# Softmax normalised on the outputs of the value product, with the values' PSUM in another bank

## The chip, the cores and the metric

The kernel runs on one core of one Trainium2 chip. The metric is the device time of one execution in microseconds (us); less is better. TensorE (PE in the profile) multiplies matrices into PSUM, VectorE (DVE) and ScalarE (ACT) work element by element, GpSimd (POOL) and SyncE (SP) issue the transfers here.

## What is computed

One layer of a streaming encoder on 512 frames with 1,024 channels, in float32: a norm, one projection into three branches and their gates, the branches, a merge, and a feed-forward block. Branches A and C are softmax attentions with 8 heads of 64 value channels; branch B is a gated recurrence. What matters here is the softmax of A and C:

```python
s = jnp.einsum('bqhd,bkhd->bhqk', q_blk, k_band).astype(jnp.float32) * scale + bias
s = jnp.where(valid[None, None], s, -jnp.inf)
p = jax.nn.softmax(s, axis=-1).astype(v.dtype)
return jnp.einsum('bhqk,bkhd->bqhd', p, v_band)
```

Each query of each head has one sum of exponentials. The probabilities may be divided by it before the product with the values, or the product's output after it.

## The kernel before

The work is done transposed: channels lie on the partitions, frames along the free dimension, 512 to a tile. Each float32 factor is split into a rounded high part and a rest (`split`, L209: ScalarE makes the high part, VectorE the rest), and each large product is three matmuls. The order of TensorE is written out by hand: `manual_schedule` names TensorE alone, and the other engines' order is left to the framework. Between the steps of the attentions `fill(n)` (L302) puts n units of dense work, matmuls of the projections, out of a queue; their weights are loaded by GpSimd.

Stages that matter: branch C's attention (about 66 to 170 us), branch A's (170 to 275 us), then the recurrence of branch B. `attention` (L566) serves C and A. It goes through 32 steps, 8 heads (h) by 4 blocks of 128 queries (t), plus some at the end:

- `scores_step` (L516): TensorE computes the scores `sc` of one block against the keys up to it (128, 256, 384 or 512 columns); VectorE finds the extreme `mn` (L525 in C; in A it adds the bias table in the same operation, L529); ScalarE takes the exponential into `p` and its sum over the row into `sm` (L532). VectorE makes the reciprocal `ri` (L536) and scales `p` in place (L537). This `norm` is issued at the end of the step.
- `transpose_step` (L540), two steps later (`LAG`): TensorE transposes the blocks of `p` into a PSUM tile `tp` (L545), one to four blocks; ScalarE and VectorE split them into `pTh` and `pTl` (L210, L211).
- `value_step` (L554), once per head, four steps after its last scores: eight matmuls into a PSUM tile `av` (L561), with the high parts of the values giving its upper 64 rows and the rests its lower 64; ScalarE copies the lower half to `avl` (L563), VectorE adds the halves into the head's 64 rows of the output `yc` or `ya` (L564).
- `prep`: in C, while a pair of heads runs, the next pair's keys and queries are made (`prep_c`, L672: stages 1 to 3 use the PSUM tiles `pk`, `pn` and `pq`; VectorE reads `pq` in L693 and L694). In A, `prep_a` (L789) prepares the head after next, and loads its bias table from memory (L803, SP queue), which VectorE negates (L804).

PSUM: tag `tp` has two banks, taken in turn by the transposes and by `av`; tag `up` has one, taken in C by `pk`, `pn` and `pq`; `sc` has two, `acc` (dense work) three.

Behind A's last step the recurrence starts: `set_yx` splits the outputs of C (L869), the gates' matmuls run as dense work, and elementwise steps (L924 on) prepare B's products, some of which need ScalarE's `d` (L986).

Of the kernel before, what the change touches and what calls it, by code (L numbers as in the profile page):

```python
# [9 lines left out]
F32 = mybir.dt.float32  # L10
F32R = mybir.dt.float32r
I32 = mybir.dt.int32
AF = mybir.ActivationFunctionType
ALU = mybir.AluOpType
# [4 lines left out]
P = 128  # L19
NK = D // P  # L20
NST = S // P
# [112 lines left out]
def body(tc, ap, dbg=None):  # L134
    with ExitStack() as ctx:
        _body(ctx, tc, ap, dbg or {})


def _body(ctx, tc, ap, dbgo):
    nc = tc.nc  # L140
    V, A, G, T = nc.vector, nc.scalar, nc.gpsimd, nc.tensor
# [23 lines left out]
    def pup(n="up"):  # L165
        return ps.tile([P, S], F32, tag="up", name=n, bufs=1)

    def psc(n="sc"):
        return ps.tile([P, S], F32, tag="sc", name=n)

    def ptp(n="tp"):
        return ps.tile([P, S], F32, tag="tp", name=n)

    def fqt(n):
        return base.tile([P, S], F32, tag="fq", name=n, bufs=8)

    def yt(n):
        return base.tile([P, S], F32, tag="y", name=n, bufs=4)
# [16 lines left out]
    ident = base.tile([P, P], F32, name="ident")  # L195
# [75 lines left out]
    def convert():  # L271

        load()
        if raw:
            hi, src = raw.pop(0)
            lo = ws.tile([P, 1024], F32R, tag="wl", name="wl")
            A.activation(lo, f(hi), AF.Copy, scale=-1.0)  # L277
            G.dma_start(lo, src, accum_op=ALU.add)
            loaded.append((hi, lo))
            load()  # L280
# [14 lines left out]
    def units():  # L295
        while queue:
            yield from queue.pop(0)()
            count[1] += 1
# [3 lines left out]
    def fill(n):  # L302
        for _ in range(n):
            if next(dense[0], None) is None:
                dense[0] = units()
                if not queue:
                    return
            unit[0] += 1
            while due and unit[0] >= due[0]:
                due.pop(0)  # L310
                if len(loaded) < 2:
                    convert()
# [20 lines left out]
    with ExitStack() as st_ctx:  # L333
# [10 lines left out]
        for k in range(NK):  # L344
            t = st.tile([P, S], F32, tag="xt", name="xt", bufs=8)
# [75 lines left out]
        for i in range(4):  # L421
            t = fqt(f"c{i}")
# [90 lines left out]

    yraw = {}

    def scores_step(ab, t, scores, bias):  # L516
        n = (t + 1) * P
        sc = psc("sc")
        for i, (l, r) in enumerate(scores):
            T.matmul(sc[:, :n], l[:, t * P:(t + 1) * P], r[:, :n], start=i == 0, stop=i == len(scores) - 1)  # L520
        mn = ab.tile([P, 1], F32, tag="mn", name="mn", bufs=6)
        p = ab.tile([P, S], F32, tag="p", name="p", bufs=LAG + 1)
        if bias is None:
            V.memset(sc[0:64, n - 64:n], -NEG)
            V.tensor_reduce(mn, sc[:, :n], X, ALU.min)  # L525
            src = sc
        else:
            src = bias[1].tile([P, S], F32, tag="sb", name="sb", bufs=2)
            V.tensor_tensor_reduce(src[:, :n], sc[:, :n], bias[0][:, S - n:], 1.0, 3.0e38,  # L529
                                   ALU.add, ALU.min, accum_out=mn)  # L530
        sm = ab.tile([P, 1], F32, tag="sm", name="sm", bufs=6)
        A.activation(p[:, :n], src[:, :n], AF.Exp, bias=mn, scale=-1.0, accum_out=sm)  # L532
        ri = ab.tile([P, 1], F32, tag="ri", name="ri", bufs=6)

        def norm():
            V.reciprocal(ri, sm)  # L536
            V.tensor_scalar(p[:, :n], p[:, :n], ri, None, ALU.mult)  # L537
        return p, norm

    def transpose_step(par, t, p, pT):  # L540
        n = (t + 1) * P
        tp = ptp("tp")
        for kt in range(t + 1):
            o = kt if par == 0 else t - kt
            T.transpose(tp[:, o * P:(o + 1) * P], p[:, kt * P:(kt + 1) * P], ident)  # L545
        src = tp[:, :n].rearrange("p (k q) -> p k q", q=P)
        if par == 0:
            dh, dl = (x[:, 0:t + 1, t * P:(t + 1) * P] for x in pT)
        else:
            dh, dl = (bass.AP(tensor=x.tensor, offset=x.offset + (4 - t) * S,  # L550
                              ap=[list(x.ap[0]), [S + P, t + 1], [1, P]]) for x in pT)
        split(dh, dl, src)

    def value_step(ab, h, v2, pT, y):  # L554
        par = h % 2
        av = ptp("av")
        for kt in range(NST):
            w = v2[kt][:, h, :]
            for i, x in enumerate(pT):
                r = x[:, kt, kt * P:] if par == 0 else x[:, 4 - kt, :(NST - kt) * P]  # L560
                T.matmul(av[:, kt * P:], w, r, start=kt == 0 and i == 0, stop=kt == NST - 1 and i == 1)  # L561
        lo = ab.tile([64, S], F32, tag="avl", name="avl", bufs=1)
        A.copy(lo, av[64:128])  # L563
        V.tensor_tensor(y[par * 64:(par + 1) * 64], av[0:64], lo, ALU.add)  # L564

    def attention(ab, ops, prep, v2, pT, ys, na, nb, nd, lag=LAG):  # L566


        pend, vals = [], []
        order = [(h, t) for h in range(8) for t in range(NST)]  # L570
        for i in range(len(order) + lag + 2):
            norm = None
            if i < len(order):
                h, t = order[i]
                p, norm = scores_step(ab, t, *ops(h))
                pend.append((h, t, p))
            fill(na[i % len(na)] if i < len(order) else nd)
            if vals and (i % 2 or i >= len(order)):
                h = vals.pop(0)
                value_step(ab, h, v2, pT, ys[h // 2])  # L580
            if len(pend) > lag or (i >= len(order) and pend):
                h, t, p = pend.pop(0)
                transpose_step(h % 2, t, p, pT)
                if t == NST - 1:
                    vals.append(h)
            if norm:
                norm()
            if i < len(order):
                prep(*order[i])
            fill(nb[i % len(nb)] if i < len(order) else nd)  # L590
        assert not pend and not vals

    with ExitStack() as at_ctx:
        ab = at_ctx.enter_context(tc.tile_pool(name="attn", bufs=2, reuse_waits="tile"))
        pT = (ab.tile([P, 5, S], F32R, tag="pTh", name="pTh", bufs=1),
              ab.tile([P, 5, S], F32R, tag="pTl", name="pTl", bufs=1))
# [5 lines left out]
        with ExitStack() as c_ctx:  # L602
# [28 lines left out]
            v2 = []  # L631
            for s in range(NST):
# [3 lines left out]
                t = ab.tile([P, 8, P], F32R, tag="v2", name="v2", bufs=4)  # L636
# [19 lines left out]
            ys = [yt("yc") for _ in range(4)]  # L656
# [56 lines left out]
            for stage in range(4):  # L713
                prep_c(0, stage)
                fill(TUNE['c1'] if stage < 3 else TUNE['c2'])

            attention(ab, lambda h: ready(h % 2), next_c, v2, pT, ys, TUNE['ca'], TUNE['cb'], TUNE['cd'])
            for pr in range(4):
                dbg('yc', ys[pr], pr)
# [11 lines left out]
        with ExitStack() as a_ctx:  # L731
            app = a_ctx.enter_context(tc.tile_pool(name="apool", bufs=2, reuse_waits="tile"))
            v2 = []
            for s in range(NST):
                t = ab.tile([P, 8, P], F32R, tag="v2", name="v2a", bufs=4)
# [5 lines left out]
            ys = [yap.tile([P, S], F32, tag="ya", name="ya", bufs=4) for _ in range(4)]  # L741
# [47 lines left out]
            def prep_a(h):  # L789
# [20 lines left out]
            prep_a(1)  # L810
            fill(TUNE['a0'])
            attention(ab, lambda h: aops[h], lambda h, t: prep_a(h + 2) if t == 3 and h < 6 else None, v2, pT, ys,
                      TUNE['aa'], TUNE['ab'], TUNE['ad'])
            for pr in range(4):
# [4 lines left out]
    with ExitStack() as h_ctx:  # L819
# [11 lines left out]
        for i in range(LEAD + 1):  # L831
            a = hp.tile([P, 2, 256], F32R, name=f"qbh{i}", bufs=1)
# [321 lines left out]
    with ExitStack() as f_ctx:  # L1154
        fp = f_ctx.enter_context(tc.tile_pool(name="ffn", bufs=2, reuse_waits="tile"))

        def fw(n):
            return fp.tile([P, S], F32, tag="fw", name=n, bufs=3)
# [27 lines left out]
        for half in range(2):  # L1186
            rT = []
            for j in range(16):
# [3 lines left out]
                t = fw("t")  # L1192
# [10 lines left out]
            for m in range(NK):  # L1203
                pz = acc("p2")
                gemm(pz, stream(ap['w_ff2'][2 * half, m], eng=V), rT, NK, stop=half == 1)
                if half == 0:
                    gemm(pz, stream(ap['w_ff2'][1, m], eng=V), rT[8:], NK, start=False)
                    t = act.tile([P, S], F32, tag="act", name="y0")
# [36 lines left out]
        for sh in range(2):  # L1245
            n = slice(sh * 256, sh * 256 + 256)
# [33 lines left out]
```

## Time and profile before

| | |
|---|---|
| median of 3 runs | 961.58 us (961.29 to 964.99) |
| the profiled execution | 962.54 us |
| its span, first to last instruction | 960.8 us |
| mean granted clock of TensorE | 0.991 |
| TensorE, VectorE, ScalarE, GpSimd busy | 919.2, 595.2, 494.5, 183.2 us |

In rows of a timeline stand the start in us, the duration in us, the engine, the line, the operation, output <- inputs, shapes, and how many instructions the row merges; in brackets the idle time of the engine before it and the instruction that ended that. PE is the matmuls, PEld the loading of their stationary operand. Rows by windows give the stretch, its length, and for each engine the busy time with the number of instructions; then the granted clock (PEclk), the share of the DMA engines, and GB/s.

### The profile page before, as it was taken

What the parts mean: (1) busy time and instruction counts of PE and PEld (TensorE: products, weight loads), DVE (VectorE), ACT (ScalarE), POOL (GpSimd) and SP (SyncE); (2) the same over time, 40 slices, a digit from 0 to 9 for tenths busy, and PEclk for the clock granted to TensorE, in tenths of its full rate; (3) what the DMA queues carried; (4) which work ended last, traced back from release to release, by engine and by line L of the source; (5) the groups of instructions that cost most, each with busy time, mean ns of one, the idle gap of its engine ahead of it and who ended that gap; (6) DMA issues with size and microseconds to landing.
All of it is one profiled execution on the core that took longest, in us unless ns stands there. A gap on an engine that the chain in (4) does not pass through costs nothing.

```text
span 960.8 us, 12589 instructions
## 1 busy us (share of the span) xinstructions
PE 919.2 (96%) x4682; PEld 774.6 (81%) x4682; DVE 595.2 (62%) x1134; ACT 494.5 (51%) x911; POOL 183.2 (19%) x248
## 2 busy tenths in 40 slices
PE   8889999988998999999999999999999999999995
PEld 6578898977877788888778888888888888888995
DVE  6488888777878969788562554544322234446745
ACT  7557778777766667667552443443322234342311
POOL 4422101111144434342122013000000000000032
PEclk9999999999999999999999999999999999999998
DMA  6865445655666474758689623223223232322402
GB/s 198 212 136 124 89 82 114 138 116 121 139 131 134 102 165 104 161 125 193 136 209 203 158 87 101 97 88 110 88 97 100 88 110 88 100 97 88 154 1 88
DMA packets 37181, 117.04 MB, mean 122 GB/s; under 512 B 4416, under 2 KB 8656, under 8 KB 37120
## 3 DMA queue, kind: packets, MB, share of 16 engines
q0 software_dynamic: 18496, 67.17, 33.3%
q1 hardware_dynamic: 18624, 49.06, 15.8%
q8 instruction: 37, 0.61, 0.3%
q14 instruction: 24, 0.20, 0.1%
HBM read 114.05 MB, written 2.16 MB: 121 GB/s over the span
## 4 chain that ended last, share of the span: by engine, by line
PE 69%; DVE 14%; issue 7%; DMA 4%; ACT 3%; POOL 2%; SPq 0%; DVEq 0%; POOLq 0%; ACTq 0%
PE p L226 12%; PE p L224 12%; PE p L225 12%; PE pg L323 3%; PE pg L319 3%; PE pg L321 3%; PE pj L323 2%; PE pj L319 2%; PE pj L321 2%; DMA bias<-in_rel 2%; PE sc L520 2%; PE po L225 2%; PE po L226 2%; PE po L224 2%; PE tp L545 1%
## 5 line engine op out<-in xcount | busy, mean ns | idle before, releaser
L220 DVE TENSOR_TENSOR wl<-wr,wh 128x1024 fp32r<-128x1024 f32 x66 | 80.8, 1224 | 144.7 <-ACT wh L219 140.6
L219 ACT CAST wh<-wr 128x1024 fp32r<-128x1024 f32 x66 | 69.5, 1053 | 173.9 <-PE p L225 136.4
L224 PE MATMUL p<-x2h,wh 128*128 128x512 f32 x256 | 100.0, 391 | 0.0
L226 PE MATMUL p<-x2h,wl 128*128 128x512 f32 x256 | 99.6, 389 | 0.0
L225 PE MATMUL p<-x2l,wh 128*128 128x512 f32 x256 | 99.6, 389 | 0.0
L277 ACT ACTIVATE wl<-wh 128x1024 fp32r<-128x1024 f32 x64 | 67.8, 1059 | 49.7 <-PE pg L323 28.1
L224 PE MATMUL p<-rh,wh 128*128 128x512 f32 (+1 forms) x224 | 83.7, 374 | 0.0
L225 PE MATMUL p<-rl,wh 128*128 128x512 f32 (+1 forms) x224 | 83.7, 374 | 0.0
L226 PE MATMUL p<-rh,wl 128*128 128x512 f32 (+1 forms) x224 | 83.7, 374 | 0.0
L323 PE MATMUL pg<-xgh,wl 128*128 128x512 f32 x192 | 76.9, 401 | 0.6 <-DMA wl<-in_w_g 0.6
L1261 POOL TENSOR_TENSOR xres<-xres,cst 128x256 f32<-128x256 f32 x16 | 13.1, 822 | 335.7 <-ACT fss L1256 309.6
L319 PE MATMUL pg<-xgh,wh 128*128 128x512 f32 x192 | 76.7, 400 | 0.0
L321 PE MATMUL pg<-xgl,wh 128*128 128x512 f32 x192 | 76.4, 398 | 0.0
L319 PE MATMUL pj<-xgh,wh 128*128 128x512 f32 x160 | 64.6, 404 | 2.6 <-ACT c L427 2.6
L321 PE MATMUL pj<-xgl,wh 128*128 128x512 f32 x160 | 65.4, 408 | 0.0
L323 PE MATMUL pj<-xgh,wl 128*128 128x512 f32 x160 | 64.0, 400 | 1.3 <-DMA wl<-in_w_aqk 1.3
L225 PEld LDWEIGHTS p<-x2l,wh 128*128 128x128 f32 x256 | 48.1, 188 | 10.2 <-issue 0.2
L224 PEld LDWEIGHTS p<-x2h,wh 128*128 128x128 f32 x256 | 48.1, 188 | 10.1 <-issue 0.2
L226 PEld LDWEIGHTS p<-x2h,wl 128*128 128x128 f32 x256 | 48.1, 188 | 10.0
L225 PEld LDWEIGHTS p<-rl,wh 128*128 128x128 f32 x224 | 42.2, 188 | 7.5
L226 PEld LDWEIGHTS p<-rh,wl 128*128 128x128 f32 x224 | 42.2, 188 | 7.5
L224 PEld LDWEIGHTS p<-rh,wh 128*128 128x128 f32 x224 | 42.2, 188 | 7.4
(380 smaller groups left out, 2398.0 us busy)
## 6 DMA issues: line engine op xcount, KB each, us to landing
wr<-in_w_ff SPq DMA_DIRECT2D x64, 512.0 KB, 3.3
wh<-in_w_g POOLq DMA_DIRECT2D x24, 512.0 KB, 4.0
wl<-in_w_g POOLq DMA_DIRECT2D x24, 512.0 KB, 5.9
wh<-in_w_br POOLq DMA_DIRECT2D x12, 512.0 KB, 3.7
wl<-in_w_br POOLq DMA_DIRECT2D x12, 512.0 KB, 5.7
wh<-in_w_aqk POOLq DMA_DIRECT2D x8, 512.0 KB, 4.5
wl<-in_w_aqk POOLq DMA_DIRECT2D x8, 512.0 KB, 6.6
wr<-in_w_out SPq DMA_DIRECT2D x8, 512.0 KB, 3.3
```

Source lines behind the costliest of these rows:

```text
L219: A.copy(hi[:, :n], r[:, :n])
L220: (eng or G).tensor_tensor(lo[:, :n], r[:, :n], f(hi[:, :n]), ALU.subtract)
L224: T.matmul(out, wh, xh, start=start, stop=False, **kw)
L225: T.matmul(out, wh, xl, start=False, stop=False, **kw)
L226: T.matmul(out, wl, xh, start=False, stop=stop, **kw)
L277: A.activation(lo, f(hi), AF.Copy, scale=-1.0)
L319: T.matmul(out, wh, xh, start=start, stop=False, **kw)
L321: T.matmul(out, wh, xl, start=False, stop=False, **kw)
L323: T.matmul(out, wl, xh, start=False, stop=stop, **kw)
L520: T.matmul(sc[:, :n], l[:, t * P:(t + 1) * P], r[:, :n], start=i == 0, stop=i == len(scores) - 1)
L545: T.transpose(tp[:, o * P:(o + 1) * P], p[:, kt * P:(kt + 1) * P], ident)
L1261: G.tensor_tensor(x2[m][:, n], x2[m][:, n], g_fin[:, m:m + 1].to_broadcast([P, 256]), ALU.mult)
```

## The change

The sums of a pair of heads are kept in one tile, one column for each block and head. `p` is no longer scaled. With the second head's value product of each pair, VectorE makes the 8 reciprocals of 128 queries and repeats each 64 times along the free dimension (`rw`, in the buffer of `avl`). Three steps later `norm` transposes the four blocks of `rw` on TensorE into a PSUM tile `rb` of tag `tp`, which then holds for each output row and query its reciprocal, and VectorE multiplies the pair's output with it. `av` takes the bank of tag `up` in place of one of tag `tp`. What is left in `norms` behind the last step is done there.

```diff
+    sums = {}
+    def scores_step(ab, h, t, scores, bias):
         n = (t + 1) * P
+        if h % 2 == 0 and t == 0:
+            sums[h // 2] = ab.tile([P, NST, 2], F32, tag="sm", name="sm", bufs=3)
...
-        sm = ab.tile([P, 1], F32, tag="sm", name="sm", bufs=6)
-        A.activation(p[:, :n], src[:, :n], AF.Exp, bias=mn, scale=-1.0, accum_out=sm)
-        ri = ab.tile([P, 1], F32, tag="ri", name="ri", bufs=6)
-
-        def norm():
-            V.reciprocal(ri, sm)
-            V.tensor_scalar(p[:, :n], p[:, :n], ri, None, ALU.mult)
-        return p, norm
+        A.activation(p[:, :n], src[:, :n], AF.Exp, bias=mn, scale=-1.0, accum_out=sums[h // 2][:, t, h % 2:h % 2 + 1])
+        return p
...
     def value_step(ab, h, v2, pT, y):
         par = h % 2
-        av = ptp("av")
+        av = pup("av")
...
         V.tensor_tensor(y[par * 64:(par + 1) * 64], av[0:64], lo, ALU.add)
+        if par:
+
+            ri = ab.tile([P, NST, 2], F32, tag="ri", name="ri", bufs=2)
+            V.reciprocal(ri, sums.pop(h // 2))
+            rw = ab.tile([P, NST, 2, 64], F32, tag="avl", name="rw", bufs=1)
+            V.tensor_copy(rw, ri.unsqueeze(3).to_broadcast([P, NST, 2, 64]))
+
+            def norm():
+                rb = ptp("rb")
+                for t in range(NST):
+                    T.transpose(rb[:, t * P:(t + 1) * P], rw[:, t].rearrange("p a d -> p (a d)"), ident)
+                V.tensor_tensor(y, y, rb, ALU.mult)
+            return norm
...
         for i in range(len(order) + lag + 2):
-            norm = None
...
             if vals and (i % 2 or i >= len(order)):
                 h = vals.pop(0)
-                value_step(ab, h, v2, pT, ys[h // 2])
+                norm = value_step(ab, h, v2, pT, ys[h // 2])
+                if norm:
+                    norms.append((i, norm))
...
-            if norm:
-                norm()
+            if norms and i > norms[0][0] + 2:
+                norms.pop(0)[1]()
...
+        for _, norm in norms:
+            norm()
```

More of the change, by code (lines that the diff above doesn't have):

```diff
@@ L514, in _body @@
     yraw = {}
-    def scores_step(ab, t, scores, bias):
+    sums = {}
+    def scores_step(ab, h, t, scores, bias):
         n = (t + 1) * P
+        if h % 2 == 0 and t == 0:
+            sums[h // 2] = ab.tile([P, NST, 2], F32, tag="sm", name="sm", bufs=3)
         sc = psc("sc")
@@ L564, in value_step @@
         V.tensor_tensor(y[par * 64:(par + 1) * 64], av[0:64], lo, ALU.add)
+        if par:
[9 more added lines that the diff above has]
+            return norm
     def attention(ab, ops, prep, v2, pT, ys, na, nb, nd, lag=LAG):
-        pend, vals = [], []
+        pend, vals, norms = [], [], []
         order = [(h, t) for h in range(8) for t in range(NST)]
         for i in range(len(order) + lag + 2):
-            norm = None
             if i < len(order):
                 h, t = order[i]
-                p, norm = scores_step(ab, t, *ops(h))
-                pend.append((h, t, p))
+                pend.append((h, t, scores_step(ab, h, t, *ops(h))))
             fill(na[i % len(na)] if i < len(order) else nd)
```

## The prediction

> **What bounds the kernel now.** I read the page's busy shares and its chain first, then the busy time by engine in the two stretches in which the two attentions run (branch C from 66 to 170 us, branch A from 170 to 275 us).
>
> ```profile
> span 960.8 us, 12589 instructions
> ...
> PE 919.2 (96%) x4682; PEld 774.6 (81%) x4682; DVE 595.2 (62%) x1134; ACT 494.5 (51%) x911; POOL 183.2 (19%) x248
> ...
> PE 69%; DVE 14%; issue 7%; DMA 4%; ACT 3%; POOL 2%; SPq 0%; DVEq 0%; POOLq 0%; ACTq 0%
> ```
> ```profile
> core 0: us, PE busy (x) PEld busy (x) DVE busy (x) ACT busy (x) POOL busy (x), PEclk, DMA share, GB/s
> 66.00:170.00 104.00, 100.45 (x615) 88.44 (x614) 88.68 (x234) 75.31 (x171) 18.40 (x22) 1.00 0.51 110
> 170.00:275.00 105.00, 96.44 (x586) 84.53 (x585) 79.99 (x240) 78.23 (x170) 19.51 (x28) 1.00 0.61 128
> ```
>
> TensorE is the bound, in the whole and in both stretches: it is idle for 3.6 us of C's 104 and for 8.6 us of A's 105. VectorE is busy for 88.7 and 80.0 us, so work taken from it is worth something only where TensorE waits for it. The groups by line, for 66 to 275 us, say where that is (the columns: count | busy us, mean ns | idle of the engine before them, and who ended it).
>
> ```profile
> L545 PE MATMUL tp<-ident,p 128*128 128x128 f32 x160 | 28.7, 278 | 9.8 <-DVE ya L564 5.6 <-DVE yc L564 2.1 <-DVE p L537 0.7
> ```
>
> The transposes of the probabilities wait for L564, the last reader of a value product: 2.1 us in C and 5.6 us in A, eight waits. The value product `av` and the transposes `tp` take turns in the same two banks, so the second transpose step after `av` needs the bank that L564 reads.
>
> **What the change removes from VectorE and adds to it.**
>
> ```profile
> L537 DVE TENSOR_SCALAR p<-p,ri 128x128 f32<-128x128 f32 (+1 forms) x64 | 24.6, 384 | 1.5
> ...
> L536 DVE RECIPROCAL ri<-sm 128x1 f32<-128x1 f32 x64 | 10.1, 159 | 10.2 <-ACT p L532 9.6
> ...
> L801 DVE CAST kt<-kt 64x512 fp32r<-64x512 f32 x8 | 3.4, 422 | 0.2
> ...
> L804 DVE TENSOR_SCALAR bias<-bias 128x256 f32<-128x256 f32 x8 | 2.2, 280 | 8.1 <-DMA bias<-in_rel 8.1
> ```
>
> Out go 64 reciprocals and 64 scalings, 34.7 us. In come, for each of 8 pairs of heads, one reciprocal (0.16), one copy of 512 columns (0.42 by L801, at most 0.69, which a 512-column operation on PSUM takes below; I take 0.42, since L801 is also a copy within SBUF) and one product with PSUM of 512 columns (0.69): 1.27 each, 10.2 us. The 24.5 us less are no term of the sum by themselves. ScalarE's sums go into another tile at the same cost: nothing. No DMA is added or moved.
>
> **What it adds to TensorE.** 32 transposes of 128 by 128, four at a time. The timeline of TensorE shows a step with four:
>
> ```profile
> 194.56 0.39 PE L323 MATMUL pj<-xgh,wl 128*128 128x512 f32 x1
> 194.79 0.40 PE L520 MATMUL sc<-kt,qt 128*128 128x256 f32 x2
> 195.02 0.60 PE L545 MATMUL tp<-ident,p 128*128 128x128 f32 x4
> 195.38 0.48 PE L319 MATMUL pj<-xgh,wh 128*128 128x512 f32 x1
> ```
>
> Matmuls of 512 columns follow each other every 0.23 us. From the end of `sc` (195.19) to the end of the next one (195.86) there are 0.67 us, so four transposes cost 0.44 us: 3.5 us for 32. By the same spacing an idle time in this view stands for 0.16 us more (0.39 less 0.23), because the next matmul could have begun before the last one's end.
>
> **Branch C.** The four waits for L564 go: 2.1 + 4 x 0.16 = 2.7 us gained. Nothing is late behind them, because the split that the next transposes need follows L564 directly. Four groups of transposes cost 1.8 us. Two new meetings have to be priced. First, `av` now waits until VectorE has read `pq` in the bank of C's preparation:
>
> ```profile
> 111.16 0.69 DVE L694 TENSOR_TENSOR qr<-pq,sinT 64x512 f32<-64x512 f32 x1
> ...
> 113.04 0.39 PE L561 MATMUL av<-pTh,v 128*128 128x512 f32 x1
> ```
>
> L694 ends 1.2 us before `av` starts. The new product (0.69) comes in front of it and a reciprocal and a scaling (0.54) leave, so 1.05 us remain: cost nothing. If that cover is gone, each microsecond later is one of TensorE. Second, `rb` takes a bank of the transposes right behind the one-block transpose of its step, so it waits for the split of the step before, which until now had one step more. In two of the three pairs that split is done; in the third it isn't:
>
> ```profile
> 154.85 0.27 PE L545 MATMUL tp<-ident,p 128*128 128x128 f32 x1
> ...
> 155.56 0.68 DVE L211 TENSOR_TENSOR pTl<-tp,pTh 128x512 fp32r<-128x512 f32 x1
> ```
>
> Held in this order that is a wait of 1.3 us; the new reciprocal and copy ahead of it add 0.58, three scalings with reciprocals that stood ahead of it (3 x 0.54) leave. I take 0.3, from 0 to 1.3. C's last `rb` has 18 dense units between it and its `av` (three fills of 6), which cover the copy; without them it would cost what A's tail does, below. C together: 2.7 - 1.8 - 0.3 = 0.6 us gained.
>
> **Branch A.** Here VectorE stands still at L804 until a bias table has landed (8.1 us in the L804 row above), and L564 and the split stand behind it. For head 1:
>
> ```profile
> 193.48 0.55 PE L545 MATMUL tp<-ident,p 128*128 128x128 f32 x3 [0.64 <-DVE ya L564]
> ...
> 205.43 0.28 PE L226 MATMUL pv<-wh,xgl 128*128 128x256 f32 x1
> 207.79 0.55 PE L545 MATMUL tp<-ident,p 128*128 128x128 f32 x3 [2.08 <-DVE ya L564]
> ...
> 209.84 0.63 PE L545 MATMUL tp<-ident,p 128*128 128x128 f32 x4 [0.55 <-DVE ri L536]
> ...
> 212.80 0.27 PE L545 MATMUL tp<-ident,p 128*128 128x128 f32 x1
> ```
> ```profile
> 206.73 0.29 DVE L804 TENSOR_SCALAR bias<-bias 128x256 f32<-128x256 f32 x1 [2.78 <-DMA bias<-in_rel]
> 207.05 0.69 DVE L564 TENSOR_TENSOR ya<-av,avl 64x512 f32<-64x512 f32 x1
> ...
> 209.28 0.42 DVE L211 TENSOR_TENSOR pTl<-tp,pTh 128x256 fp32r<-128x256 f32 x1
> ...
> 212.80 0.69 DVE L211 TENSOR_TENSOR pTl<-tp,pTh 128x512 fp32r<-128x512 f32 x1
> ```
>
> After the change the three-block transpose runs without a wait at 205.55 (the last matmul before it, of 256 columns, keeps TensorE half of 0.23 us). The four-block one is ready 1.34 us later (207.79 to 209.84, less its own 0.55 and 0.16), at 206.9, and needs the split of 209.28. That split stays behind L804 and L564, and as head 1 closes a pair it now has a reciprocal and a copy (0.58) in front of it: it ends at 210.3, and TensorE is 0.5 us later than before. At 212.80 `rb` then wants the bank whose split ends at 213.49, plus 0.58, less a reciprocal and a scaling (0.5): 213.6, against TensorE's 213.4. So head 1: 0.5 + 0.2 + 0.44 = 1.1 us lost. Head 3 goes the same way:
>
> ```profile
> 234.80 0.55 PE L545 MATMUL tp<-ident,p 128*128 128x128 f32 x3 [2.64 <-DVE ya L564]
> ...
> 236.35 0.60 PE L545 MATMUL tp<-ident,p 128*128 128x128 f32 x4
> ...
> 239.90 0.30 PE L545 MATMUL tp<-ident,p 128*128 128x128 f32 x1 [0.74 <-DVE p L537]
> ```
> ```profile
> 234.78 0.42 DVE L211 TENSOR_TENSOR pTl<-tp,pTh 128x256 fp32r<-128x256 f32 x1
> ...
> 240.01 0.69 DVE L211 TENSOR_TENSOR pTl<-tp,pTh 128x512 fp32r<-128x512 f32 x1
> ```
>
> The four-block transpose would come at 233.55 and gets its split at 235.2 + 0.58 = 235.8, 0.55 earlier than before; the wait at 239.90 goes too. But `rb` needs the split that ends at 240.70, now 240.8, and TensorE is past it at 241.2 where it was past the one-block transpose at 240.0: 1.2 us lost. Head 0's wait (0.64 + 0.16) goes for good, the third pair costs 0.44. The eighth wait, at the end of A, hands over to the split behind it and gives nothing. A: 0.8 - 1.1 - 1.2 - 0.4 = 1.9 us lost.
>
> **A's tail.** The last norm has no fill in front of it (`ad=0`):
>
> ```profile
> 272.64 0.27 PE L561 MATMUL av<-pTl,v2a 128*128 128x128 f32 x1
> ...
> 272.95 0.58 ACT L563 COPY avl<-av 64x512 f32<-64x512 f32 x1 [2.08 <-PE av L561]
> ...
> 273.57 0.68 DVE L564 TENSOR_TENSOR ya<-av,avl 64x512 f32<-64x512 f32 x1 [1.97 <-ACT avl L563]
> ```
>
> The copy `rw` reuses `avl`'s buffer and starts after L564, at 274.25; it ends at 274.7, and TensorE, which went on at once, stands 1.9 us and works 0.44. But TensorE waits further on anyway, for the elementwise work of the next stage:
>
> ```profile
> 301.22 0.36 PE L224 MATMUL sl<-qbh,kxh 128*128 128x256 f32 x1 [2.66 <-ACT d L986]
> ```
> ```profile
> 298.00:300.00 2.00, 0.56 (x3) 0.14 (x1) 2.00 (x2) 0.60 (x3) 1.92 (x4) 1.00 0.59 68
> ...
> 302.00:304.00 2.00, 2.00 (x8) 1.57 (x7) 1.97 (x4) 0.88 (x1) 0.82 (x1) 0.55 0.71 254
> 304.00:306.00 2.00, 2.00 (x7) 1.59 (x6) 0.98 (x3) 1.69 (x5) 0.05 (x1) 0.59 0.71 72
> ```
>
> VectorE is full there, so that wait ends later by the 1.27 us added to VectorE, and TensorE's own delay is absorbed by it: the price is 1.3 us (from 1.3 to 2.3). The wait shrinks from 2.8 to about 1.8 us. After it the granted clock was 0.55 and 0.59 for two slices of 2 us, which cost 0.9 + 0.8 = 1.7 us; after waits of 2.08 and 2.64 us in A the clock stayed at 1.00. So a shorter wait here may save 1.7 us; I take half, 0.8. [...]
>
> **Sum**: 0.6 - 1.9 - 1.3 + 0.8 = 1.8 us slower. The profiled execution took 962.54 us (span 960.8 and 1.7 around it), 0.96 above the median of 961.58; the difference goes on either: 964.3 for a profiled run like it, 963.4 for the median.
>
> **The rivals.** About 0.5%, 4.8 us, is what a measurement of this kernel can tell from no change.
> 1. The waits really go: VectorE, 24.5 us lighter, gets another order in which the splits come ahead of L804. Then 7.7 + 1.3 for L564 and 0.9 + 0.7 for the two waits on L536 and L537 are gained, 10.6, less 3.5 and 1.3: 5.8 faster, 955.8. For it: no order of VectorE is written in the kernel. Against it: the bias lands no earlier, as its load is issued behind TensorE's scores.
> 2. Slower: the wait at the four-block transpose becomes long enough to cost the clock. In head 1 TensorE would stand from 206.9 to 210.3, 3.4 us, longer than the 2.66 that did it at 301. If the clock falls there and in head 3, 1.7 each, and the saving of 0.8 doesn't come, it is 1.8 + 3.4 + 0.8 = 6.0 slower, 967.6. It decides from a standstill of some 2.7 us. [...] Against it: waits of 2.08 and 2.64 left the clock at 1.00.
> 3. The shared bank holds `av` back: the product stands ahead of L693 and L694 when VectorE is late by more than the 1.05 us. As long as the waits that it replaces in C, 0.8 for three pairs, it is 2.4 more: 965.8.
>
> **How the numbers follow.** The order as held: 0.50, with 961 to 966.5 from the bounds (the clock saved in full or not, 0 or 1.3 at 155 us, the tail at 2.3, the copy at 0.69 eight times). Rivals 1, 2 and 3: 0.20, 0.20 and 0.10. Faster by over 0.5% takes most of rival 1: 0.15. Slower by over 0.5% takes most of rival 2, some of rival 3 and the upper end of the forecast: 0.25. The rest is 0.60. The range goes from rival 1's value to above rival 2's: 956 to 968.5.
>
> **What would show it.** Right: no transposes waiting for L564; in A waits of 2 to 3.5 us at four-block transposes, released by a split or by what follows it; `rb` waiting for a split in heads 3 and 5; a standstill of about 2 us behind A's last `av`; a shorter wait near 301 us. Wrong: A's stretch without waits above 1 us (rival 1), a granted clock under 1.00 between 205 and 245 us (rival 2), `av` waiting for L693 or L694 (rival 3), or groups of four transposes that cost much over 0.44 us.

## The result and the profile after

| | before | after |
|---|---|---|
| median of 4 runs | 961.43 us (960.89 to 964.99) | 971.85 us (968.98 to 975.58) |
| ratio, 95% interval | | 1.0093 [1.007, 1.0116] |
| the profiled execution, its span | 962.54, 960.8 us | 972.06, 970.3 us |
| mean granted clock | 0.991 | 0.984 |

The change is slower by 0.9%: little, but the interval excludes no change. The forecast was 963.4 us with a range of 956.0 to 968.5: slower by 1.8 us was the right side, but most of the loss is not in its sum. From the page of the changed kernel:

```profile
PE 928.0 (96%) x4714; PEld 783.4 (81%) x4714; DVE 576.7 (59%) x1030; ACT 493.5 (51%) x911; POOL 183.8 (19%) x248
```

VectorE lost 18.5 us of work and the kernel became 9.5 us longer. TensorE has 32 instructions more and 8.8 us more of busy time, far over the 3.5 us of 32 transposes at the prediction's price; at a halved clock the same matmuls count as longer: a `pj` of 512 columns takes 0.63 us at 171.06, where the granted clock is 0.50, and 0.39 us at 176.04, where it is 1.00. Added up over windows of 2 us, TensorE's busy time times (1 - granted clock) is 5.1 us before and 10.3 after, so about 5 of the 9.5 us are lost clock.

The groups of the transposes, 60 to 275 us (count | busy us, mean ns | idle before them, by whom ended):

```profile
L543 PE MATMUL tp<-ident,p 128*128 128x128 f32 x157 | 28.0, 275 | 4.8 <-DVE pTl L211 4.3 <-DVE sc L528 0.4
...
L573 PE MATMUL rb<-ident,rw 128*128 128x128 f32 x28 | 4.8, 297 | 4.6 <-DVE rw L568 3.2 <-DVE pTl L211 1.4
```

The addition of the two halves, `ya` and `yc` (L564 before, L562 now), releases no transposes any more. In its place stand the split `pTl`, and `rw`, the repeated reciprocals.

Where the 9.5 us arise is read best by following one fixed instruction of each stage through both kernels. These are the last matmul of a value product in C (heads 0 and 7) and in A (heads 0, 1, 2 and 4), the first matmul `sl` of the next stage, and one of its `po`; first before, then after. A's head 7 (272.64) and the `sl` at 301.22 of before stand in the prediction.

```profile
90.47 0.27 PE L561 MATMUL av<-pTl,v 128*128 128x128 f32 x1
...
166.09 0.28 PE L561 MATMUL av<-pTl,v 128*128 128x128 f32 x1
...
189.35 0.28 PE L561 MATMUL av<-pTl,v2a 128*128 128x128 f32 x1
...
202.11 0.28 PE L561 MATMUL av<-pTl,v2a 128*128 128x128 f32 x1
...
216.98 0.28 PE L561 MATMUL av<-pTl,v2a 128*128 128x128 f32 x1
...
244.15 0.27 PE L561 MATMUL av<-pTl,v2a 128*128 128x128 f32 x1
...
295.62 0.28 PE L224 MATMUL sl<-qbh,kxh 128*128 128x256 f32 x1
...
332.77 0.28 PE L224 MATMUL po<-qbh,kxh 128*128 128x256 f32 x1
```
```profile
89.44 0.27 PE L559 MATMUL av<-pTl,v 128*128 128x128 f32 x1
...
165.41 0.28 PE L559 MATMUL av<-pTl,v 128*128 128x128 f32 x1
...
194.45 0.28 PE L559 MATMUL av<-pTl,v2a 128*128 128x128 f32 x1
...
206.37 0.28 PE L559 MATMUL av<-pTl,v2a 128*128 128x128 f32 x1
...
223.96 0.28 PE L559 MATMUL av<-pTl,v2a 128*128 128x128 f32 x1
...
249.25 0.27 PE L559 MATMUL av<-pTl,v2a 128*128 128x128 f32 x1
...
278.14 0.27 PE L559 MATMUL av<-pTl,v2a 128*128 128x128 f32 x1
...
308.32 0.28 PE L224 MATMUL sl<-qbh,kxh 128*128 128x256 f32 x1
...
311.10 0.29 PE L224 MATMUL sl<-qbh,kxh 128*128 128x256 f32 x1
...
342.80 0.28 PE L224 MATMUL po<-qbh,kxh 128*128 128x256 f32 x1
```

The differences of the starts give the delay at each point, and their steps give what each stage cost:

| up to | delay, us | step, us | what lies in it |
|---|---|---|---|
| C, head 0 | -1.0 | -1.0 | the start, ahead of the change |
| C's last `av` | -0.7 | +0.3 | branch C |
| A, head 0 | +5.1 | +5.8 | C's tail |
| A, head 1 | +4.3 | -0.8 | the wait of head 0 |
| A, head 2 | +7.0 | +2.7 | the wait of head 1 |
| A, head 4 | +5.1 | -1.9 | the waits of head 3 |
| A, head 7 | +5.5 | +0.4 | the third pair |
| `sl` | +12.7 | +7.2 | A's tail |
| `sl` behind the wait of 2.66 us | +9.9 | -2.8 | that wait is gone |
| `po` | +10.0 | +0.1 | the clock behind that wait, saved; another loss, below |

The first row is no effect of the change. The code up to there is the same, and the time lies in a wait of TensorE for `c` (L427), 2.61 us at 33.33 before and 1.70 us at 32.41 after; other runs differ there by a microsecond or more too (e4's TensorE is 1.2 us later than before at that point). Counted from C's head 0, `po` is 11.0 us late.

Two places carry the loss: the tails of the two attentions.

**C's tail.** The timeline of TensorE, then of VectorE:

```profile
165.41 0.28 PE L559 MATMUL av<-pTl,v 128*128 128x128 f32 x1
168.89 1.09 PE L573 MATMUL rb<-ident,rw 128*128 128x128 f32 x4 [3.20 <-DVE rw L568]
169.63 0.78 PE L319 MATMUL pj<-xgh,wh 128*128 128x512 f32 x1
```
```profile
167.00 0.69 DVE L562 TENSOR_TENSOR yc<-av,avl 64x512 f32<-64x512 f32 x1
167.72 0.69 DVE L211 TENSOR_TENSOR v2a<-avn,v2a 128x512 fp32r<-128x512 f32 x1
168.33 0.42 DVE L568 COPY rw<-ri 128x512 f32<-128x512 f32 x1
```

No dense unit stands between `av` and `rb`. The three calls of `fill(6)` found the queue empty; the next `pj` belongs to the next stage and follows `rb` in TensorE's order. Before the change it followed `av` (166.09) at once, at 166.21. VectorE is late besides: as before the change it splits A's values here (`v2a`), 1.29 us ahead of L562 and 0.69 between L562 and the copy. And behind the standstill the clock, 1.00 in the windows from 160 to 168 us, falls to about half (the windows' last three columns are the granted clock, the DMA share and GB/s):

```profile
168.00:170.00 2.00, 1.11 (x5) 1.14 (x6) 1.34 (x3) 0.00 (x0) 0.00 (x0) 0.51 0.88 174
170.00:172.00 2.00, 2.00 (x6) 1.52 (x6) 0.69 (x1) 0.00 (x0) 0.00 (x0) 0.50 0.00 0
172.00:174.00 2.00, 2.00 (x8) 1.61 (x6) 0.00 (x0) 0.00 (x0) 0.00 (x0) 0.50 0.00 0
174.00:176.00 2.00, 2.00 (x8) 1.64 (x8) 0.30 (x2) 0.49 (x2) 0.00 (x0) 0.78 0.00 0
```

From 168.89 to 176 TensorE has work throughout and gets 0.57, 1.00, 1.00 and 1.56 us' worth of full clock in 7.1 us: 3.0 us lost, beside the 3.36 us of standing and 0.44 of work.

**A's tail.** TensorE's row, VectorE's, and GpSimd's first and last of the clearing operations that run one behind the other:

```profile
282.80 1.09 PE L573 MATMUL rb<-ident,rw 128*128 128x128 f32 x4 [4.39 <-DVE rw L568]
```
```profile
279.78 2.87 DVE L568 COPY rw<-ri 128x512 f32<-128x512 f32 x1
```
```profile
278.36 0.96 POOL L842 MEMSET sT<- 128x1024 f32 x1 [1.68 <-PE av L559]
...
282.05 0.32 POOL L954 MEMSET d<- 128x128 f32 x1
```

The copy that takes 0.36 to 0.42 us at the other seven places (0.42 in C's tail, above) takes 2.87 us here. TensorE stands for 4.39 us, and works at half the clock after it:

```profile
282.00:284.00 2.00, 1.20 (x5) 1.24 (x6) 0.73 (x2) 2.00 (x8) 1.49 (x4) 0.50 0.00 0
284.00:286.00 2.00, 2.00 (x6) 1.52 (x6) 2.00 (x4) 0.03 (x1) 0.00 (x0) 0.50 0.00 0
286.00:288.00 2.00, 2.00 (x8) 1.52 (x7) 2.00 (x7) 0.00 (x0) 0.78 (x1) 0.62 0.00 0
```

Counted as in C, 2.4 us of clock are lost (0.6, 1.0 and 0.8).

### The profile page after: what moved, and what is told of

Its sections match the earlier page's. It is cut to its first block, busy times and chain, and to the rows that moved or that the text cites. A ratio compares the mean times of both kernels' runs of the same rounds, so it can differ in the third digit from the quotient of the medians.

```text
span 970.3 us, 12585 instructions
## 1 busy us (share of the span) xinstructions
PE 928.0 (96%) x4714; PEld 783.4 (81%) x4714; DVE 576.7 (59%) x1030; ACT 493.5 (51%) x911; POOL 183.8 (19%) x248
## 4 chain that ended last, share of the span: by engine, by line
PE 69%; DVE 14%; ACT 6%; issue 4%; DMA 4%; POOL 1%; SPq 0%; DVEq 0%; POOLq 0%; ACTq 0%
PE p L226 12%; PE p L225 12%; PE p L224 12%; PE pj L323 3%; PE pj L319 3%; PE pj L321 2%; PE pg L323 2%; PE pg L319 2%; PE pg L321 2%; PE sc L524 2%; DVE qbl L211 2%; PE po L225 2%; PE po L226 2%; PE po L224 2%; DMA bias<-in_rel 2%
## 5 line engine op out<-in xcount | busy, mean ns | idle before, releaser
L225 PEld LDWEIGHTS p<-x2l,wh 128*128 128x128 f32 x256 | 48.0, 188 | 10.3 <-issue 0.2
```

The costliest lines, as they stand in the source:

```text
L225: T.matmul(out, wh, xl, start=False, stop=False, **kw)
```

## The experiments

The ratios are to the kernel before, with 95% intervals; less is faster. Line numbers move by a few lines from kernel to kernel.

| | edit | ratio |
|---|---|---|
| the change | | 1.0093 [1.007, 1.0116] |
| e1 | the last pair of each branch scales `p` as before | 0.9994 [0.9975, 1.0012] |
| e2 | unused matmuls ahead of each branch's last `rb` | 1.005 [1.0031, 1.0069] |
| e5 | last pair's `rw` made ahead of its `av` | 1.0006 [0.9985, 1.0028] |
| e10 | as e5, in C alone | 1.002 [0.9997, 1.0043] |
| e11 | `rw` by a product instead of a copy | 1.0099 [1.007, 1.0127] |
| e3 | three buffers for the bias instead of two | 1.008 [1.005, 1.011] |
| e6 | all bias tables loaded at A's start | 1.0042 [1.0025, 1.0059] |
| e8 | e5 and e6 together | 0.9951 [0.9935, 0.9967] |
| e4 | the kernel before, `av` in `up` | 0.9977 [0.9962, 0.9992] |
| e9 | the kernel before, tables early | 0.9937 [0.9916, 0.9958] |
| e7 | the kernel before, both | 0.9911 [0.9881, 0.9942] |

The theory at first: the tails cost the time, because nothing covers the way from the last `av` over `rw` to `rb`. The rival: the cost is spread over the transposes, the copies and the shared bank.

**e1: the tails undone.**

```diff
-        return p
+        if h < 6:
+            return p, None
+        def norm_p():
+            V.reciprocal(r1, sums[3][:, t, h % 2:h % 2 + 1])
+            V.tensor_scalar(p[:, :n], p[:, :n], r1, None, ALU.mult)
+        return p, norm_p
...
-        if par:
+        if par and h < 7:
```

> The changed kernel, but the last pair of heads of each branch scales its probabilities as before, so that no reciprocals are turned behind a branch's last value product. Theory: the 9.5 us are mostly the two standstills behind the last products (3.4 us in C, 4.6 in A) with the half clock that follows each (about 2.9 and 2.7 us, partly taken up by a wait that A's recurrence had anyway): the time falls by 9 to 11 us, to 961 to 963. Rival, that the cost is spread evenly (transposes, copies, the shared bank): a quarter of it goes, 968.5 to 970.

963.06 us against 963.13: the whole loss is gone, within the interval, although three of four pairs still normalise on the outputs and head 1 in A still waits (2.83 us). The theory holds; the rival falls.

**e2: work in the gap.** It adds matmuls whose result nobody uses, so its time has them in it.

```diff
+        busy = psc("busy")
+        for _ in range(16):
+            T.matmul(busy, xg[0][0][:, :P], xg[0][0], start=True, stop=True)
         for _, norm in norms:
             norm()
```

> The changed kernel with 16 unused matmuls of 512 columns (3.7 us of TensorE work) in front of the last turn of each branch, where TensorE stands still. The standstills stay as long; only TensorE isn't idle in them. Theory that the half clock is a large part of the cost: 4 to 6 us less than the changed kernel, 966 to 968, and a granted clock near 1.00 behind both. Rival, that only the standstills count: no less than the changed kernel, 971 to 973.

969.62 us, between the theory's 966 to 968 and the rival's 971 to 973. The stretches behind the two `rb`, which start at 174.53 and 287.47 in this run:

```profile
174.00:182.00 8.00, 8.00 (x44) 6.82 (x43) 2.92 (x10) 1.60 (x5) 0.48 (x1) 1.00 0.12 23
288.00:294.00 6.00, 6.00 (x28) 4.96 (x28) 4.89 (x11) 1.63 (x5) 2.12 (x3) 1.00 0.01 3
```

The clock is 1.00 where it was 0.50. The added matmuls fill the standstill, so that time is spent either way; the 0.4% between this kernel and the change, about 4 us, is the clock's part. It is somewhat under half of the tails' 9 us, but roughly known: the two intervals almost touch. (Between 34 and 60 us, ahead of everything changed, TensorE lost about 4 us more of clock in this profiled run than in the change, so only the tails are read from it.)

**e5: the copy earlier.** The last pair's reciprocals are ready before its value product, since they need only the sums. Their buffer can't be `avl`'s then; it is one of `p`'s.

```diff
+        if h == 7:
+            rw = repeat("p", LAG + 1)
         av = pup("av")
...
-            rw = ab.tile([P, NST, 2, 64], F32, tag="avl", name="rw", bufs=1)
-            V.tensor_copy(rw, ri.unsqueeze(3).to_broadcast([P, NST, 2, 64]))
+            if h < 7:
+                rw = repeat("avl", 1)
```

> The changed kernel, but the last pair of each branch has its reciprocals repeated ahead of its value product, in a buffer of the probabilities' ring, so that the copy needn't wait for the last reader of the value product. Theory: at both tails only the chain of copy behind product behind ScalarE's copy makes TensorE wait; then the standstills of 3.4 and 4.6 us and the half clock behind them go, and the time is that of the kernel before within 0.3% (ratio 0.997 to 1.003). Rival, that the tails cost through the turning and the product with the output themselves: half or more of the 0.9% stays.

962.77 us against 963.3. In C's tail `rb` follows `av` without a gap:

```profile
166.54 0.27 PE L567 MATMUL av<-pTl,v 128*128 128x128 f32 x1
166.65 0.62 PE L578 MATMUL rb<-ident,rw 128*128 128x128 f32 x4
```

In A's tail too `rb` follows `av` (272.56, then 272.68). The eight transposes of both tails remain; the 0.9 us that they cost by the prediction's price are less than the interval can show. So it was the place of the copy.

**e10: the same in C alone**, to part the two tails.

```diff
-        if h == 7:
+        if h == 7 and late['early']:
             rw = repeat("p", LAG + 1)
```

> The change, with the reciprocals' copy of the last pair made ahead of its value product in branch C only; A's tail stays as changed. It tells the two tails apart. Theory: C's tail costs its standstill (3.2 + 0.16 us), the four transposes' 0.44 and the half clock after it (about 3 us), 6 in all less what a later wait absorbs, so this is 4 to 6 us faster than the change: ratio to the kernel before 1.003 to 1.005, C's tail at clock 1.00, A's standstill of 4.4 us and its half clock still there, and A's tail is left with 3 to 5 us, less than it loses in place, because the wait near 301 us and its clock loss go in return. Rival: A's longer standstill is the dearer one and C's is mostly absorbed: ratio 1.007 or more.

966.42 us, ratio 1.002; the number was to be 1.003 to 1.005, which the interval still holds. C's tail has no standstill and a clock of 1.00; A's is as it was (`rb` waits 4.39 us). So C's tail is the dearer one: about 0.7% of the change's 0.9%. A's is dearer on the spot, 7.2 against 5.8 us, but 2.8 us of it come back in the wait for `d` that it makes superfluous. The split is rough: each of the two intervals is 0.2% wide to either side, and by e10 and e5 A's tail is left with about 0.1%, where the rows leave 4.4 us.

**e11: a product instead of the copy**, to find out why the copy took 2.87 us.

```diff
-            V.tensor_copy(rw, ri.unsqueeze(3).to_broadcast([P, NST, 2, 64]))
+            V.tensor_tensor(rw, ri.unsqueeze(3).to_broadcast([P, NST, 2, 64]),
+                            one1.unsqueeze(2).unsqueeze(3).to_broadcast([P, NST, 2, 64]), ALU.mult)
```

> The change, with the reciprocals repeated by a product with one in place of a copy. Everything else is the same. Theory: A's last copy took 2.87 us, where the other seven took 0.36 to 0.42, because a copy within SBUF is held up by GpSimd's memsets that run beside it, which a product of two SBUF operands is not: it takes about 0.7 us at A's tail as at the other seven places, the standstill there falls from 4.39 to about 2.2 us, and the time is 1 to 3 us below that of the change (ratio 1.006 to 1.009; 7 products are 0.3 us longer than the copies). Rival: VectorE was held up there by something else (its sums' semaphores, the shared buffer of avl, the transfers): the product then takes over 2 us there as well, and the standstill is 4 us or more.

VectorE at A's tail, and the last of GpSimd's clearings there:

```profile
279.99 0.69 DVE L568 TENSOR_TENSOR rw<-ri,one 128x512 f32<-128x512 f32 x1
```
```profile
282.26 0.34 POOL L955 MEMSET d<- 128x128 f32 x1
```

The product runs through in 0.69 us amid the same clearing operations, and TensorE waits 2.21 us instead of 4.39. The copy takes 2.87 to 2.89 us at this place in every profiled run that keeps it there (e2, e3, e6 and e10 too). So at this place it is the copy, as a kind of operation, that takes longer. In e5, where the copy of A's last pair runs at 267.95 us, ahead of `av` and of the clearing (from 272.79 us), it takes 0.43 us; the product of the same size takes 0.69 with the clearing beside it. These times agree with the theory that the clearing held up the copy and not the product, but how it did so isn't shown, and no run takes the clearing away. In the change the copy ended at 282.65, 0.3 us after the last of the eight clearings, and not behind the one (0.53 us) that it met. The time is a miss: 972.38 us, ratio 1.0099, where 1.006 to 1.009 was expected. TensorE's standstill at A's tail is 2.2 us shorter, but over the runs nothing of that arrives; each of the other seven products is 0.3 us longer than its copy, and where the rest goes stays open. The interval, 1.007 to 1.0127, reaches into the expected range, so a gain of 1 to 3 us isn't excluded either.

**e3 and e6: head 1's wait.** It is the largest wait inside A: TensorE's row, two windows behind it, and what VectorE does ahead of the split.

```profile
214.84 0.66 PE L543 MATMUL tp<-ident,p 128*128 128x128 f32 x4 [3.57 <-DVE pTl L211]
```
```profile
216.00:218.00 2.00, 2.00 (x10) 2.00 (x10) 2.00 (x8) 1.50 (x3) 0.86 (x1) 0.50 0.00 0
218.00:220.00 2.00, 2.00 (x14) 2.00 (x14) 0.91 (x4) 1.39 (x5) 0.01 (x1) 0.69 0.63 82
```
```profile
211.92 0.29 DVE L817 TENSOR_SCALAR bias<-bias 128x256 f32<-128x256 f32 x1 [3.34 <-DMA bias<-in_rel]
...
212.85 0.68 DVE L562 TENSOR_TENSOR ya<-av,avl 64x512 f32<-64x512 f32 x1
```

The copy (0.35 us) follows at 213.64 and the split at 214.37.

e3, a third buffer:

```diff
-                bias = app.tile([P, S], F32, tag="bias", name="bias", bufs=2)
+                bias = app.tile([P, S], F32, tag="bias", name="bias", bufs=3)
```

> The changed kernel with three buffers in place of two for A's bias table, so that its load doesn't wait for the scores of the head before. Theory: head 1's wait of 3.7 us and its half clock (1.7) go, as VectorE no longer stands still in front of the split: 966 to 967.5. Rival, that the split is late through the new copy and VectorE's queue and not through the load: under 1.5 us less, 970.5 or more.

A miss: 971.94 us. VectorE still waits 1.89 us for this table and TensorE 2.48, behind which the clock stays at 1.00. SyncE's queue holds the loads back nearly as before: from 190 to 230 us they wait behind `mn` (L533) for 37.0 us in three waits, in the change for 39.1. A free buffer doesn't change that; which of the two it waits for, its buffer or its place in the queue, this run doesn't say.

e6 takes the loads out of that place:

```diff
+            rel = app.tile([P, 8, 256], F32, name="rel", bufs=1)
+            for h in range(8):
+                nc.sync.dma_start(rel[:, h], ap['rel'][h])
...
-                nc.sync.dma_start(bias[:, 256:], ap['rel'][h])
-                V.tensor_scalar(bias[:, 256:], bias[:, 256:], -1.0, None, ALU.mult)
+                V.tensor_scalar(bias[:, 256:], rel[:, h], -1.0, None, ALU.mult)
```

> The changed kernel with all eight bias tables of branch A loaded at its start, so that VectorE has no transfer to wait for in the middle of A. Theory: head 1's wait (3.7 us) and the half clock behind it (1.7) go, and part of head 3's: 4 to 6 us less than the changed kernel, ratio to before 1.003 to 1.006. Rival, that the split is late through the copy and VectorE's queue: ratio 1.008 or more.

967.04 us, 0.5% below the change. Its group of `tp` waits for only 0.6 us, that of `rb` mainly for `rw` in the tails (7.6 of 9.8 us):

```profile
L543 PE MATMUL tp<-ident,p 128*128 128x128 f32 x160 | 28.4, 275 | 0.6 <-DVE sc L528 0.4 <-DVE pTl L211 0.2
```

**e4, e9, e7 and e8: what was good in it.** e4 is the kernel before with one word changed, e9 the kernel before with e6's edit, e7 has both; e8 is the change with e5's and e6's edits.

```diff
-        av = ptp("av")
+        av = pup("av")
```

> The kernel before with only the values' PSUM moved to the bank of branch C's preparation; the probabilities are scaled as before. Theory: in C the four waits for the product's last reader (2.7 us) go at no cost, in A head 0's (0.8) and part of head 3's (1.1), while head 1's moves to the four-block transpose and may cost the clock (1.7): 957 to 960. Rival, that the bank itself is what costs, through products waiting for the preparation: 962.5 or more.

961.08 us: 0.23% faster, the sign right and the size under the expected. C's waits are gone; in A they move, as the prediction had it, to the next transposes (1.78, 1.11 and 1.79 us).

> The kernel before with all bias tables of branch A loaded at A's start, the value product left in the transposes' banks. It splits the gain of the fastest version (0.9911) in two. Theory: each of the two edits takes away waits of its own. Then C's waits for L564 (2.1 us in the view, 2.7 with 0.16 each) and head 0's in A stay, and only A's waits behind the bias (2.08, 2.64, 0.74, and the clock loss after 2.66 us only if it moves) go: 957 to 960, ratio 0.994 to 0.998, and the trace still shows about 2 us of transposes waiting for L564 in C. Rival: the tables alone do it, since they give VectorE its time back: ratio 0.992 or less.

957.23 us, 0.9937: the tables alone are worth 0.6%. The waits for `yc` in C stay:

```profile
L545 PE MATMUL tp<-ident,p 128*128 128x128 f32 x160 | 28.5, 277 | 2.8 <-DVE yc L564 2.1 <-DVE ya L564 0.3 <-DVE ri L536 0.2
```

> The kernel before with the values' PSUM in the bank of the preparation and all bias tables loaded early; the probabilities are scaled as before. Theory: the waits at heads 1 and 3 that were left when only the bank moved (1.9, 1.3 and 1.9 us) go: ratio to before 0.992 to 0.996. Rival, that eight loads at A's start only move the wait, or that VectorE's queue makes it: 0.997 or more.

953.8 us, 0.9911: the lowest of all, a little under the expected 0.992, and faster than both kernels. The two gains add up (0.23 and 0.63 against 0.89%).

> Both mendings in the changed kernel: the early copy at the tails and the early tables. If each takes its own part (0.9% for the tails, 0.4 to 0.6% for head 1), the ratio to before is 0.993 to 0.997, and the change would then be about as fast as the bank and the tables alone. If the waits are one and the same stock that only moves, 0.999 or more.

958.37 us against e7's 953.8 on the same chip in the same series: with both mendings the changed kernel beats the one before, and is still 0.4% behind e7, which scales `p`; the two intervals overlap a little, so this isn't quite certain. The 32 transposes would account for 3.5 us of it by the prediction's price, and its group of `rb` waits 2.2 us for splits; no run takes the two apart. No gain from VectorE's 18.5 us shows here.

## Why the prediction was wrong

**The step that failed** is "C's last `rb` has 18 dense units between it and its `av` (three fills of 6), which cover the copy; without them it would cost what A's tail does". The code calls the fills, but the queue was empty. The trace of before could have told it:

```profile
162.79 0.60 PE L545 MATMUL tp<-ident,p 128*128 128x128 f32 x4
164.38 0.50 PE L561 MATMUL av<-pTh,v 128*128 128x512 f32 x1 [0.99 <-ACT pTh L210]
...
185.03 0.30 PE L545 MATMUL tp<-ident,p 128*128 128x128 f32 x1 [0.63 <-DVE pTl L211]
```

Between C's last transpose and its last `av` the code calls two fills, and TensorE stands idle with no unit in the rows: nothing was left already then. The step was to cost nothing; it cost 5.8 us on the spot (e10: about 0.7%, some 7 us over the runs). That is 3.4 of standing, 0.4 of work and 3.0 of clock, less the wait at 185.03 (0.63 + 0.16), which is gone: 6.0 by this count. Nor would it "cost what A's tail does", put at 1.9 us of standing: the splits of A's values on VectorE made it longer, and the prediction left them out.

**A's tail** had the right mechanism and a wrong size. The standstill was put at 1.9 us with a copy of 0.42; the copy took 2.87 us beside GpSimd's clearing, and the standstill was 4.39. The prediction took the copy from others (L801, 0.42 each, at 151.6 to 244.3 us), which had no clearing beside them: in the kernel before, the clearing starts at 272.87. And no price was put on the clock after a standstill in either tail, although the prediction priced it at 301 us and in rival 2. On the spot it is 7.2 us against 2.3: 4.55 of standing (4.39 + 0.16), 0.4 of work and 2.4 of clock, 7.4 by this count. What was to come back did: the wait for `d` is gone altogether (2.8 us), and with it its lost clock.

**Branch C** was to gain 0.6 and lost 0.3 between its first and its last value product. The four waits for L564 are gone as said. What was mis-sized is the wait of the third pair's `rb`: taken at 0.3, it is 1.03 (0.87 + 0.16), which alone brings the sum to -0.1. In e1 the same `rb` waits 1.48 us, so it isn't a fixed cost.

**A's inside** was to lose 1.9 and lost 0.4, by errors that cancel. Head 0 gained 0.8 and the third pair lost 0.4, as said. Head 1 was to lose 1.1: it lost 2.7, because rival 2 came true there, a standstill of 3.57 us (3.4 in the rival) and a clock of 0.50 and 0.69 behind it. Head 3 was to lose 1.2 and gained 1.9: there rival 1 came true. VectorE got another order:

```profile
237.55 0.68 DVE L562 TENSOR_TENSOR ya<-av,avl 64x512 f32<-64x512 f32 x1
238.27 0.42 DVE L211 TENSOR_TENSOR pTl<-tp,pTh 128x256 fp32r<-128x256 f32 x1
...
239.78 0.29 DVE L817 TENSOR_SCALAR bias<-bias 128x256 f32<-128x256 f32 x1 [0.75 <-DMA bias<-in_rel]
```

L562 and the split run ahead of the bias, not behind it; before, the bias ran at 233.14 and L564 at 234.06. The prediction held that order of VectorE fixed though nothing in the kernel fixes it, and named as much in the rival.

**Rival 3** didn't occur: no `av` waits for the shared bank, and e4 gains by it.

## What to carry to other kernels

Work that may be absent is no cover: look in the trace for the units that a fill is to bring, at the very place, before they are counted. At the end of both attentions the way from the last matmul back into TensorE was bare (standstills of 3.20 and 4.39 us), and what such a way needs should be made before that matmul where it can (e5: one copy moved, and the loss is gone within the interval). A long standstill of TensorE cost its length and in both tails the clock behind it, which at A's tail was half as much again (2.4 for 4.55 us) and at C's almost as much (3.0 for 3.36); and the 18.5 us taken off VectorE showed no gain of their own (e8's 958.37 us against e7's 953.8).

## What was not expected of the hardware

A copy within SBUF of 0.42 us took 2.87 us while GpSimd cleared memory, and a product in its place 0.69 (e11).

In these runs the length of a standstill doesn't by itself settle the clock. Those of 2.80, 2.83, 2.94 and 3.57 us at head 1 (e10, e1, e11 and the change) took it to between 0.50 and 0.56 in the lowest window of 2 us; the same wait for `d` took it in the kernel before (2.66 us; 0.55 and 0.59) and left it at 1.00 in e9 (2.67 us). A wait of 0.76 us for `kxl`, at 365.17 before and at 375.20 after, was followed by 0.50 before (the window from 368 us) and by 1.00 after. Two waits ahead of `po`, 0.28 and 1.53 us before, 0.47 and 1.53 us after, left it at 1.00 before, and it fell after; in e3, with 0.49 and 1.53 us, it stayed. The windows from TensorE's return on, before and after:

```profile
330.00:332.00 2.00, 2.00 (x12) 1.75 (x12) 1.95 (x3) 1.64 (x3) 0.85 (x2) 1.00 0.18 51
```
```profile
338.00:340.00 2.00, 1.77 (x8) 1.57 (x9) 2.00 (x4) 1.20 (x2) 1.28 (x2) 0.68 0.05 4
340.00:342.00 2.00, 2.00 (x6) 1.58 (x5) 1.13 (x3) 1.95 (x5) 0.86 (x1) 0.50 0.80 262
```

That is the other loss in the table of delays (1.6 us): it takes back the clock saved behind the vanished wait for `d`. What decides whether a standstill costs the clock isn't shown: waits of nearly equal length (2.66 and 2.67 us; 0.76 and 0.76; 1.53 behind 0.47 and behind 0.49) came out either way, and no run here moved one standstill in time with all else held.
